# One transposed half tile copied out of PSUM by another engine, in a kernel whose order is set by a planner: tanh(x w1) * (x w2)

## The chip, the cores and the metric

The kernel runs on one core of a Trainium2 chip. The time is the device time of one execution in microseconds. Before the change three executions took 297.3, 297.45 and 297.87 us, so the median is 297.45 us.

In this document PE is TensorE (matmuls; PEld is its weight load), DVE is VectorE, ACT is ScalarE, POOL is GpSimd and SP is SyncE, which here only issues DMAs.

## The reference

```python
def setup_inputs():
    batch, m, k, n = 16, 512, 1024, 768
    return {
        "x": np.random.randn(batch, m, k).astype(np.float32),
        "w1": np.random.randn(k, n).astype(np.float32),
        "w2": np.random.randn(k, n).astype(np.float32),
    }

def reference(x, w1, w2):
    y1 = np.matmul(x, w1)
    y2 = np.matmul(x, w2)
    return (np.tanh(y1) * y2).astype(np.float32)
```

There are 8192 rows of x (64 row tiles of 128), a depth of 1024 (8 slices of 128, in two halves of 4), and 2 x 768 columns of weights. The weights are seen as three blocks of 512 columns: block a is the first 512 columns of w1, block b the first 512 of w2, and block g holds the last 256 of w1 and the last 256 of w2 side by side.

## The kernel before

**Two ways of multiplying.** The first four row tiles (HEAD = 4) are multiplied plainly: per row tile, block and depth slice one matmul of 128 x 128 by 128 x 512 in fp16. An op named `m2a3` is row tile 2, block a, slice 3. The other 60 row tiles go in 20 groups of three ("triples"). Three row tiles in two depth halves, times three blocks in two halves, would take 18 products of four matmuls each; the kernel takes 15, from sums and differences of halves of x (ops `S..`, on VectorE) and of halves of the weights (ops `B..`, on VectorE, made once). A product is an op like `p6.0`, product 6 of triple 0; each has four matmuls, and copies (`copy..`, `seed..`, on ScalarE) and additions (`add..`, on VectorE) join the products in PSUM. Tanhs (`th..`, `t..`) are on ScalarE and the final multiplications (`mu..`, `m0.i` to `m2.i`, `mh..`) on VectorE.

**How data comes in.** At the start SP and ScalarE issue loads of x and of the weights as fp32 into staging space (`arena`, `early_x`), and GpSimd loads block b and later x straight into fp16. Casts to fp16 follow: `ca0` to `ca7` (block a, VectorE), `cg0` on VectorE and `cg1` to `cg7` on ScalarE (block g), `cx20` (row tile 2, half 0) and so on (VectorE). The weight loads of block g come behind those of x and block a on SP's queue; one pair of them serves both `cg0` and `cg4`.

**How x is transposed.** From row tile 7 on, a DMA does it (line 387). The first seven row tiles are transposed by TensorE: op `PT20` is row tile 2, half 0, four matmuls against an identity (line 380) into a PSUM bank. Then `e20` copies the bank to `xT` (lines 366 on ScalarE and 368 on VectorE), and `m2a0` and its like can read it. Row tile 3 has a tile of its own, `xT_kept`; the first halves of row tiles 0 and 1 are transposed in fp32.

**Other work.** `D0` to `D63` on ScalarE (line 390) sum the absolute values of each row tile; each is an ACTIVATE followed by a read-out of the sum. `f1` to `f5` near the end test all those sums for a range: `f1` to `f3` on VectorE, one small matmul `f4` (line 495), and `f5` on VectorE; if they fail a general path runs, which they don't here. POOL and SP order x loads, transposing DMAs and stores.

**What sets the order.** Nothing is scheduled on the chip: each engine runs its queue in order. The queues are written by a planner (class `Planner`, lines 75 to 223) when the program is built. Every op has one cost per engine that may run it, a due time and the ops it needs; the planner walks through time, gives each op to an engine and a PSUM bank when both are free, and the order in which it does so is the program's order. The order of the products on TensorE is fixed by a list; all else follows from the costs. A change of one cost can therefore change which engine takes another op, which bank it gets and in which order the queues stand.

The costs of the copies that this change touches are in `by_pe` (line 587), called for each half of the first seven row tiles.

Of the kernel before, what the change touches and what calls it, by code (L numbers as in the profile page):

```python
# [74 lines left out]
class Planner:  # L75
# [9 lines left out]
    def op(self, name, engines, due, needs, fn, *args, behind=(), issued=(), chains=(), xfer=0.0, latency=None, seeds=False,  # L85
           lands=None, hold=0.0):
        assert name not in self.ops, name
        self.ops[name] = dict(engines=engines, due=due, needs=[n for n in needs if n], behind=[n for n in behind if n], issued=[n for n in issued if n], fn=fn, args=args,
                              chains=chains, xfer=xfer, latency=latency, seeds=seeds, lands=lands, hold=hold)
        for c in chains:  # L90
            self.chains.setdefault(c, {"left": 0, "bank": None, "end": 0.0, "act": 0.0, "dve": 0.0})["left"] += 1
# [135 lines left out]
def kernel(  # L227
# [16 lines left out]
    HEAD = 4  # L244
# [66 lines left out]
    op = plan.op  # L311
# [245 lines left out]
    for n, what in enumerate(by_pool):  # L557
# [7 lines left out]
        else:  # L565
            mt, h = int(what[1]), what[2:]
# [20 lines left out]
    def by_pe(mt, h, due, load):  # L587
        fp32 = (mt, h) in FP32
        op(f"PT{mt}{h}", {"pe": 0.44 if fp32 else 0.24}, due, [load], transpose_pe, mt, h, ("T", mt, h), chains=[("T", mt, h)])
        op(f"e{mt}{h}", {"dve": 0.6 if fp32 else 0.45, "act": 0.5} if mt < HEAD else {"act": 0.5}, due + 0.4, [f"PT{mt}{h}"], evacuate, mt, h, ("T", mt, h),  # L590
           chains=[("T", mt, h)])

    for n, after in enumerate(("PT00", "PT10")):
# [1 line left out]
    for mt in range(HEAD):  # L595
        for h in range(2):
            if (mt, h) not in FP32:
                op(f"cx{mt}{h}", {"dve": 0.37}, lands[f"x{mt}{h}"] - 1, [f"Lx{mt}{h}"], cast_x, mt, h)
            by_pe(mt, h, lands[f"x{mt}{h}"] - 2, f"Lx{mt}{h}" if (mt, h) in FP32 else f"cx{mt}{h}")
        op(f"D{mt}", {"act": 1.05}, START + 8, [f"Lx{mt}0", f"Lx{mt}1"], abs_x, mt, hold=11 + 4 * mt)  # L600
    for mt in rows[HEAD:BY_PE]:
        for h in range(2):
            by_pe(mt, h, x_loads[mt, h][1] - 2 - 0.1 * h * (mt == HEAD + 1), x_loads[mt, h][0])
# [36 lines left out]
    for n, s in enumerate("agb"):  # L640
        for mt in range(HEAD):
            if (s, mt) == ("b", HEAD - 1):
                continue
            due, behind = (lambda n: landed[slices["agb".index(s) * KO + n]] + 0.8 + 0.02 * mt), []
            finals(mt, s, due(KO - 1) + (5.0, 3.0, 7.0)["agb".index(s)], plain(mt, s, due, behind))

    mt = HEAD - 1
# [57 lines left out]
    for i in range(TRIPLES):  # L705
# [10 lines left out]
        for o in C_OPS:  # L716
# [20 lines left out]
            mt = HEAD + 3 * i + r  # L737
            due = soonest[i, name] + LAST
# [177 lines left out]
```

## Time and profile before

| | |
|---|---|
| median of three executions | 297.45 us |
| the profiled execution | 297.16 us |
| its span, first to last instruction | 295.6 us |
| VectorE busy | 255.8 us |
| ScalarE busy | 224.4 us |
| GpSimd busy | 42.3 us |

The span is 1.56 us shorter than the execution's time; the rest lies around it. The profile's timeline gives, per row: the start in us from the span's start, the duration, the engine, the line of the kernel, the operation, the tiles written and read, the shape out and in, and in brackets how long the engine had been idle before it and what released it. A row with "x2" or more merges instructions that follow one another, and its duration is that of the run. VectorE and ScalarE instructions that follow one another overlap by about 0.1 us in these rows, and matmuls overlap more: a matmul of 512 columns shows 0.38 us and the next one starts 0.216 us later. A busy share of TensorE is thus the share of time in which some matmul was under way.

The copies and casts of one half row tile, 128 x 512, stand in the profile's groups with 586 to 587 ns (ACT COPY from PSUM, line 366), 425 ns (DVE COPY from PSUM, line 368) and 427 ns (DVE CAST from fp32, line 368).

### The profile page before, as it was taken

To read this page: it belongs to the slowest core of one execution; us is meant where nothing else is said; L and a number is where in the kernel's file an instruction comes from. 1 tells how busy PE (TensorE), PEld (TensorE's weight loads), DVE (VectorE), ACT (ScalarE), POOL (GpSimd) and SP (SyncE) were. 2 spreads that over 40 slices of the span, in tenths; PEclk is the share of its full clock that TensorE was granted. 3 is DMA by queue.
4 is the path that set the end of the run, shared out by engine and by line. 5 is a ranking of instruction groups with operands and counts; after the bars stand their busy time and mean duration, and the time that the engine had idled before them with its cause. 6 is when DMAs were issued, how large, how long until landed. Compare 5 with 4: busy or idle time off the path is not lost. (4 is left out here: it accounts for less than half of the span.)

```text
span 295.6 us, 4588 instructions
## 1 busy us (share of the span) xinstructions
PE 289.5 (98%) x1374; PEld 132.3 (45%) x1374; DVE 255.8 (87%) x552; ACT 224.4 (76%) x454; POOL 42.3 (14%) x94
## 2 busy tenths in 40 slices
PE   7999999999999999999999999999999999999994
PEld 3445444444444444444444444444444444444442
DVE  1679999999989998898989888898988889898875
ACT  2698599799878878877888888677777767778442
POOL 0065022202102102202012021020211100000000
PEclk9999999999999999999999999999999999999999
DMA  6999999999999999989999999999999999241234
GB/s 217 391 321 204 182 141 169 210 247 230 240 194 197 247 226 216 252 218 239 204 190 246 231 236 270 164 271 264 224 298 225 213 175 324 104 162 53 109 136 169
DMA packets 84858, 63.63 MB, mean 215 GB/s; under 512 B 62816, under 2 KB 67168, under 8 KB 84832
## 3 DMA queue, kind: packets, MB, share of 16 engines
q1 hardware_dynamic: 73888, 45.10, 59.7%
q0 software_dynamic: 9936, 16.65, 36.0%
q10 hardware_dynamic: 1008, 1.57, 1.5%
q8 instruction: 11, 0.18, 0.2%
q14 instruction: 15, 0.12, 0.1%
HBM read 39.85 MB, written 25.17 MB: 220 GB/s over the span
## 5 line engine op out<-in xcount | busy, mean ns | idle before, releaser
L457 PE MATMUL bank<-b,early_x 128*128 128x512 f16 x640 | 148.3, 379 | 0.0
L457 PEld LDWEIGHTS <-early_x 128*128 128x128 f16 x800 | 78.1, 98 | 94.3 <-DVE early_x L421 0.3
L467 DVE TENSOR_TENSOR bank<-bank,arena 128x512 f32<-128x512 f32 x100 | 69.6, 696 | 13.6 <-ACT arena L461 10.9
L461 ACT ACTIVATE arena<-bank 128x512 f32<-128x512 f32 x100 | 57.6, 596 | 18.1 <-PE bank L457 18.1
L475 DVE TENSOR_TENSOR o<-o,bank 128x256 f32<-128x256 f32 (+1 forms) x128 | 61.9, 516 | 7.3 <-ACT o L470 5.9
L390 ACT ACTIVATE junk<-xh 128x1024 f16<-128x1024 f16 x60 | 63.4, 1057 | 0.1
L457 PEld LDWEIGHTS <-xT 128*128 128x128 f16 x400 | 39.0, 98 | 46.9 <-issue 0.4
L457 PE MATMUL bank<-b,xT 128*128 128x512 f16 x240 | 58.3, 379 | 0.0
L470 ACT ACTIVATE o<-bank 128x256 f32<-128x256 f32 (+1 forms) x80 | 34.8, 438 | 26.0 <-DVE bank L467 22.8
L457 PE MATMUL bank<-wh,xT 128*128 128x512 f16 x160 | 41.0, 379 | 0.0
L457 PE MATMUL bank<-wh,early_x 128*128 128x512 f16 x160 | 40.9, 379 | 0.0
L362 POOL DMA_DIRECT2D xh<-in_x_dram x61 | 32.4, 540 | 16.6 <-ACT junk L390 8.6
L421 DVE TENSOR_TENSOR early_x<-early_x,xT 128x512 f16<-128x512 f16 x80 | 33.5, 420 | 0.5
L470 ACT ACTIVATE o<-arena 128x512 f32<-128x512 f32 x40 | 25.2, 629 | 7.5 <-DVE arena L467 7.5
L501 POOL CAST held<-xT 128x1 f32<-128x1 f16 x18 | 4.5, 251 | 161.3 <-DMA xT<-xh 161.3
L461 ACT ACTIVATE bank<-bank 128x512 f32<-128x512 f32 x40 | 21.4, 570 | 4.7 <-PE bank L457 3.9
L430 PE MATMUL bank<-wh,xT 128*128 128x512 f16 x72 | 19.5, 379 | 0.3
L467 DVE TENSOR_TENSOR arena<-bank,arena 128x512 f32<-128x512 f32 x20 | 13.7, 686 | 3.6 <-ACT arena L461 3.6
L421 DVE TENSOR_TENSOR early_x<-xT,xT 128x512 f16<-128x512 f16 x40 | 16.7, 418 | 0.0
L421 DVE TENSOR_TENSOR early_x<-xT,early_x 128x512 f16<-128x512 f16 x40 | 16.7, 418 | 0.0
L467 DVE TENSOR_TENSOR bank<-arena,bank 128x512 f32<-128x512 f32 x20 | 13.8, 692 | 0.1
L390 ACT ACTIVATE junk<-wh 128x768 f16<-128x768 f16 x16 | 13.6, 847 | 0.1
(51 smaller groups left out, 140.0 us busy)
## 6 DMA issues: line engine op xcount, KB each, us to landing
out_dram<-o SPq DMA_DIRECT2D x59, 384.0 KB, 5.1
xh<-in_x_dram POOLq DMA_DIRECT2D x58, 256.0 KB, 6.7
arena<-in_w_dram SPq DMA_DIRECT2D x12, 256.0 KB, 5.6
early_x<-in_x_dram SPq DMA_DIRECT2D x8, 256.0 KB, 4.9
arena<-in_w_dram ACTq DMA_DIRECT2D x4, 256.0 KB, 5.9
wh<-in_w_dram POOLq DMA_DIRECT2D x8, 128.0 KB, 5.5
xT<-xh SPq DMA_TRANSPOSE x57, 4.2
out_dram<-o SPq DMA_DIRECT2D x3, 256.0 KB, 2.5
```

Source lines behind the costliest of these rows:

```text
L362: pin(nc.gpsimd.dma_start(xh(mt)[:, cols], xf[mt][:, cols]))
L390: pin(nc.scalar.activation(junk[:, :src.shape[-1]], src, ACT.Abs, scale=scale, accum_out=sums[:, column:column + 1]))
L421: pin(engine[e].tensor_tensor(x_operand(i, v), x_operand(i, a), x_operand(i, b), OP[how]))
L430: pin(nc.tensor.matmul(bank(chain)[:, :rhs.shape[-1]], xt(mt)[:, k, :], rhs, start=first, stop=k == KO - 1, skip_group_check=True))
L457: pin(nc.tensor.matmul(place(i, dst), x_operand(i, a)[:, k, :], w_rhs(b, k), start=begins and k == 0, stop=k == KH - 1, skip_group_check=T ...
L461: pin(nc.scalar.activation(place(i, dst), place(i, src), ACT.Copy, scale=float(sign)))
L467: pin(nc.vector.tensor_tensor(place(i, dst), a, b, ALU.add if signs == (1, 1) else ALU.subtract))
L470: pin(nc.scalar.activation(out_tile(HEAD + 3 * i + r)[:, lo:lo + n], place(i, src)[:, :n], ACT.Tanh, scale=float(sign)))
L475: pin(nc.vector.tensor_tensor(o, o, place(i, src)[:, at:at + n], ALU.mult))
L501: pin(nc.gpsimd.tensor_copy(held, xt(mt)[:, 0, :1]))
```

## The change

In `by_pe`, the copy `e20` may run on VectorE only, with cost 0.45; the other copies of the first four row tiles count ScalarE's time with 0.6 in place of 0.5. The copies of row tiles 4 to 6 stay on ScalarE with 0.5.

```diff
     def by_pe(mt, h, due, load):
         fp32 = (mt, h) in FP32
         op(f"PT{mt}{h}", {"pe": 0.44 if fp32 else 0.24}, due, [load], transpose_pe, mt, h, ("T", mt, h), chains=[("T", mt, h)])
-        op(f"e{mt}{h}", {"dve": 0.6 if fp32 else 0.45, "act": 0.5} if mt < HEAD else {"act": 0.5}, due + 0.4, [f"PT{mt}{h}"], evacuate, mt, h, ("T", mt, h),
+        op(f"e{mt}{h}", {"dve": 0.45} if (mt, h) == (2, 0) else {"dve": 0.6 if fp32 else 0.45, "act": 0.6} if mt < HEAD else {"act": 0.5}, due + 0.4, [f"PT{mt}{h}"], evacuate, mt, h, ("T", mt, h),
            chains=[("T", mt, h)])
```

The order that the planner then writes differs in these places:

| engine | before | after |
|---|---|---|
| VectorE, start | cx20 ca2 cx30 ... ca7 e31 cg0 | cx20 ca2 **e20** cx30 ... ca7 cg0 |
| ScalarE, start | e10 e20 e30 e01 e60 e11 D0 copy376.0 e21 D1 tha0 cg4 tha1 tha2 cg1 cg5 tha3 cg2 cg6 cg3 cg7 D2 thg0 ... thg3 D3 e61 e40 e41 | e10 e30 e01 e60 e11 D0 e21 copy376.0 **e31 cg4 tha0** tha1 cg1 cg5 tha2 cg2 cg6 tha3 cg3 cg7 D1 thg0 ... thg3 D2 e61 **D3** e40 e41 |
| TensorE, start | m2a0 PT30 m2a1 m2a2 m0a3 PT01 m3a0 m1a3 m3a1 PT60 m3a2 PT11 m2a3 m3a3 m0a4 p7.0 | m2a0 m2a1 PT30 m2a2 m0a3 PT01 m1a3 m2a3 m3a0 PT60 m3a1 m3a2 PT11 m3a3 p7.0 m0a4 |
| TensorE, end of block a | m2a6 m0a7 m1a7 m3a4 m3a5 m3a6 m2a7 m3a7 | m2a6 m0a7 m1a7 m2a7 m3a4 m3a5 m3a6 m3a7 |
| VectorE, first triple | B29.0 S3.0 S34.0 S11.0 S35.0 add64.0 S15.0 | B29.0 **B48.0** S3.0 S34.0 S11.0 S35.0 add64.0 S15.0 |
| TensorE, first triple | m0b7 p6.0 p1.0 p12.0 m1b7 m2b7 p9.0 | m0b7 **m1b7** p6.0 p1.0 p12.0 m2b7 p9.0 |
| TensorE, near the end | p13.18 f4 p6.19 p10.19 p4.18 p5.18 p9.19 | p13.18 p6.19 p10.19 p4.18 p5.18 **f4** p9.19 |
| VectorE, near the end | f1 S34.19 f2 S35.19 f3 add60.18 f5 m0.18 add312.19 m2.18 add64.19 add8.18 | S34.19 f1 add60.18 S35.19 m2.18 m0.18 add312.19 add64.19 f2 f3 add8.18 f5 |

Beside these, neighbours change places in some triples (such as t2 with copy60, or m0 with add312), the PSUM banks of the chains are handed out differently from the first triple on (the product p10.0 takes the bank that e40 leaves, before it took that of e41), and on SP's queue the store of row tile 4 stands before the transposing DMA of row tile 16. GpSimd's queue is the same.

## The prediction

> **What bounds the kernel now.** I read the page's totals first, then a window over the long middle, then the timeline of single engines around the edits.
>
> ```profile
> span 295.6 us, 4588 instructions
> PE 289.5 (98%) x1374; PEld 132.3 (45%) x1374; DVE 255.8 (87%) x552; ACT 224.4 (76%) x454; POOL 42.3 (14%) x94
> 17.66:291.43 273.77, 273.67 (x1290) 124.81 (x1288) 247.53 (x531) 214.89 (x439) 41.62 (x88) 1.00 0.99 210
> ```
>
> The window row gives, from its left, the length of the stretch, TensorE's busy time (matmuls), weight loads, VectorE, ScalarE, GpSimd, the granted clock (1.00). From 17.66 us to its last matmul TensorE is idle for 0.10 us of 273.77. So TensorE bounds the kernel, and nothing after 17.66 can give back more than a few tenths. The edits lie before that, and they can matter in two ways only: by moving the moment at which the gapless stretch begins, or by opening holes in it.
>
> **The edit itself: e20 to VectorE, e31 back to ScalarE.** The built order has row tile 2's first copy (e20) on VectorE, between two casts; row tile 3's second copy (e31) goes the other way. Each engine keeps its count of copies.
>
> ```profile
> 8.34 0.43 DVE L368 CAST wh<-arena 128x512 f16<-128x512 f32 x1
> 8.46 0.23 PEld L380 LDWEIGHTS <-xh 128*128 128x128 f16 x4 [0.52 <-DVE xh L368]
> 8.90 0.59 ACT L366 COPY xT<-bank 128x512 f16<-128x512 f16 x1 [1.12 <-PE bank L380]
> 9.33 0.43 DVE L368 CAST xh<-early_x 128x512 f16<-128x512 f32 x1 [0.57 <-DMA early_x<-in_x_dram]
> 9.54 0.10 PEld L430 LDWEIGHTS <-xT 128*128 128x128 f16 x1 [0.62 <-ACT xT L366]
> 9.81 0.23 PEld L380 LDWEIGHTS <-xh 128*128 128x128 f16 x4 [0.18 <-DVE xh L368]
> 10.66 0.25 PEld L380 LDWEIGHTS <-xh 128*128 128x128 f16 x4 [0.29 <-DVE xh L368]
> 14.72 0.10 PEld L430 LDWEIGHTS <-xT 128*128 128x128 f16 x1 [0.21 <-issue]
> 15.25 0.10 PEld L430 LDWEIGHTS <-xT 128*128 128x128 f16 x1 [0.44 <-ACT xT L366]
> 15.98 0.42 DVE L368 COPY xT_kept<-bank 128x512 f16<-128x512 f16 x1
> 17.18 0.43 DVE L368 CAST wh<-arena 128x512 f16<-128x512 f32 x1 [0.78 <-DMA arena<-in_w_dram]
> 17.43 0.38 PE L430 MATMUL bank<-wh,xT_kept 128*128 128x512 f16 x1
> 17.66 1.24 PE L430 MATMUL bank<-wh,xT 128*128 128x512 f16 x5
> ```
>
> Row 8.90 is e20 on ScalarE, 0.59; row 15.98 is the same copy on VectorE (e31), 0.42. VectorE is idle from 8.77 to 9.33, waiting for row tile 3's data. So e20 runs there 8.90 to 9.32, and the cast behind it (row 9.33, cx30) is not delayed. The first matmul of row tile 2 (row 9.54) starts 0.16 earlier, at 9.38.
>
> Does 0.16 reach the end? In the new order one more matmul of row tile 2 stands ahead of the transposes PT30: two matmuls of 0.216 (five starts in 1.24 with 0.38 for the last) fill 9.38 to 9.81, where PT30 may start as before. Then two matmuls to 10.48, and PT01 needs the cast cx01 and cannot load before 10.66. Before, the spare matmul filled this hole and PT01 came at 10.70. So 0.04 is left of 0.16. It stays 0.04 through 15.25 (e21, now 0.04 earlier). TensorE would finish the first weight block at 17.60 instead of 17.65 (17.43 + 0.216). But the first matmul of the next block needs the cast cg0: row 17.18, which waited 0.78 for a weight load, ends 17.61, and the matmul comes at 17.66. The loads are unchanged and wait for no copy. **Head: 0**; between -0.02 (the matmul at 17.65 plus no wait) and +0.16 (the hole at 10.48 grows by the whole gain and nothing behind absorbs it). I take 0, since row 17.66 follows cg0 by the 0.05 that a released TensorE needs.
>
> [...]
>
> **e31 and the reordered ScalarE queue.** ScalarE now does e31, then the cast cg4, and only then the tanh of row tile 0.
>
> ```profile
> 16.55 0.60 ACT L433 ACTIVATE o<-bank 128x512 f32<-128x512 f32 x1 [0.30 <-PE bank L430]
> 17.17 0.62 ACT L366 CAST wh<-arena 128x512 f16<-128x512 f32 x1
> 17.69 1.08 ACT L433 ACTIVATE o<-bank 128x512 f32<-128x512 f32 x2
> 19.72 0.59 ACT L433 ACTIVATE o<-bank 128x512 f32<-128x512 f32 x1
> 21.72 1.14 ACT L366 CAST wh<-arena 128x512 f16<-128x512 f32 x2 [0.39 <-DMA arena<-in_w_dram]
> ```
>
> PT31 starts 15.43; a copy starts 0.42 behind its transposes (26.13 to 26.55, below): e31 15.85 to 16.44. Its reader, one matmul later in the order, starts 16.73: 0.24 spare. cg4 uses the same load as cg0, so it starts at 17.17 as now, and ScalarE idles 0.7 ahead of it. The displaced tanh takes 17.69; the tanhs behind it move one place each, so the casts cg1, cg5, cg2, cg6 keep their places, and the last tanh falls into the 0.39 of idle time before 21.72. **Cost 0**; without that idle time it would be one tanh's 0.5.
>
> **Two sums of absolute values and one weight sum move up.** ScalarE's D3 now stands between e61 and e40, and VectorE's B48.0 between B29.0 and S3.0.
>
> ```profile
> 25.10 1.05 ACT L390 ACTIVATE junk<-early_x 128x1024 f16<-128x1024 f32 x1
> 26.13 0.39 PE L380 MATMUL bank<-ident_h,xh 128*128 128x128 f16 x4
> 26.55 0.59 ACT L366 COPY xT<-bank 128x512 f16<-128x512 f16 x1 [0.31 <-PE bank L380]
> 27.68 1.07 ACT L366 COPY xT<-bank 128x512 f16<-128x512 f16 x2 [0.54 <-PE bank L380]
> 30.09 0.59 ACT L366 COPY xT<-bank 128x512 f16<-128x512 f16 x1 [0.51 <-PE bank L380]
> 26.21 1.29 DVE L412 TENSOR_TENSOR b<-wh 128x1024 f16<-128x1024 f16 x2
> 28.02 0.69 DVE L412 TENSOR_TENSOR b<-b,b 128x1024 f16<-128x1024 f16 x1
> 28.79 0.43 DVE L421 TENSOR_TENSOR early_x<-xT 128x512 f16<-128x512 f16 x1
> 29.13 0.42 DVE L421 TENSOR_TENSOR early_x<-xT,xT 128x512 f16<-128x512 f16 x1
> 29.61 0.76 DVE L421 TENSOR_TENSOR early_x<-early_x,xT 128x512 f16<-128x512 f16 x2
> 30.88 0.42 DVE L421 TENSOR_TENSOR early_x<-early_x,xT 128x512 f16<-128x512 f16 x1
> 28.80 1.02 PE L457 MATMUL bank<-wh,xT 128*128 128x512 f16 x4
> 31.40 0.38 PE L457 MATMUL bank<-b,early_x 128*128 128x512 f16 x1
> 35.93 0.42 DVE L421 TENSOR_TENSOR early_x<-xT 128x512 f16<-128x512 f16 x1 [0.28 <-DMA xT<-xh]
> ```
>
> D3 starts 0.48 behind e61 (two copies in 1.07), at 27.03, and holds ScalarE 1.05: e40 starts 28.08 instead of 27.68, ends 28.67; e41 ends 29.15. The product p10.0 (row 28.80) used e41's bank with no time to spare; in the new assignment it takes e40's, free at 28.72. So it starts at 28.80 still. e50 keeps 30.09.
>
> VectorE: B48.0 starts 28.62 (two such sums take 1.29, so 0.60 apart) and S3.0, which needs e41, at 29.22 instead of 28.79. From S3.0 to S15.0 (row 30.88) the rows show 2.09. Of this 0.14 is a wait for the copy e51 at row 29.61 (ops of this kind start 0.34 apart, 28.79 and 29.13), and it is gone when S3.0 is late. So S15.0 starts 29.22 + 1.95 = 31.17 and ends 31.59; p6.0 can start 31.64. TensorE has m1b7 moved ahead of p6.0, 31.40 + 0.216 = 31.62. **Stall 0.02 to 0.03.** Bounds: 0 if VectorE runs a hair faster, and 0.42 if S15.0 is late by B48.0's whole 0.69 (31.30 + 0.69 + 0.05 - 31.62). I take 0.03, which the spacing of the rows gives. The remaining 0.29 of VectorE's lateness ends at 35.93, where it now idles 0.28.
>
> [...]
>
> **The flag near the end.** The one-matmul check f4 moves behind p5.18, its input f3 behind VectorE's add64.19.
>
> ```profile
> 272.95 0.24 DVE L492 TENSOR_REDUCE count<-good 128x1 bf16<-128x80 f32 x1
> 273.56 0.70 DVE L467 TENSOR_TENSOR bank<-bank,arena 128x512 f32<-128x512 f32 x1 [0.37 <-ACT o L470]
> 276.02 0.68 DVE L467 TENSOR_TENSOR arena<-arena,bank 128x512 f32<-128x512 f32 x1
> 273.59 0.17 PE L495 MATMUL bank<-count,ones 128*128 128x8 bf16 x1
> 275.34 2.97 PE L457 MATMUL bank<-b,early_x 128*128 128x512 f16 x13
> ```
>
> TensorE reaches f4 at 275.34 + 8 x 0.216 - 0.03 = 277.04. add60.18 (row 273.56) waited for a ScalarE tanh on its bank; in the new program order it precedes that tanh, so VectorE is 0.6 ahead. A 0.34 sum comes in between it and add64.19, f5's 0.1 goes out, so add64.19 starts about 275.7; f2 and f3 behind it end 1.0 later, at 276.7. **Cost 0.** If add60.18 still waits, add64.19 starts 276.3, f3 ends 277.3, and TensorE waits 0.3.
>
> The other swaps repeat orders that this trace already runs without a hole in other triples; one store moves ahead of one transposing DMA on SP's queue, GpSimd's order is the same. I cost them at nothing, covered by the gapless row above.
>
> **Sum.** 0 + 0 + 0.03 + 0 = 0.03 on the profiled execution's 297.16, giving 297.19. That execution stands 0.29 below the median 297.45, to which the same 0.03 gives 297.48: **297.5**.
>
> **Rivals.**
> Slower: D3 in front of e40. If D3's place costs all of its 1.05 and its read-out's 0.2 instead of the 0.40 worked out, e41 ends at 28.75 + 1.24 = 29.99, S3.0 starts 30.03, S15.0 ends 32.40 and p6.0 waits until 32.45: a hole of 0.83, 298.3. It decides from S15.0 ending after 32.16, 0.57 later than worked out. For it: e40, e41, S3.0, S15.0 and p6.0 hang on one another and p6.0 has nothing to spare. Against it: ScalarE's 0.54 of idle time at row 27.68 covers half of D3.
> Flag: TensorE waits 0.3 in front of f4, 297.75; against it stands the new program order.
> Copy: e20 takes ScalarE's 0.59 on VectorE also, cx30 comes 0.16 late, and no later wait absorbs it: 297.6; against it row 15.98.
> Gain kept: cg0's load lands 0.2 earlier and the 0.16 arrives, 297.3. Nothing in the edit moves a load.
> [...]
> Faster: cg0's load lands most of a microsecond earlier, and the head's holes become worth closing. The weight-load idle times 0.62, 0.18, 0.21 and 0.44 above sum to 1.45; about half lies beside running matmuls, an estimate from matmuls of 0.38 that start 0.216 apart, so 0.7: 296.75.
>
> **How the numbers follow.** Forecast 0.63 (its own range 297.2 to 297.8), flag 0.06, copy 0.04, gain kept 0.05, full drain 0.02, slower chain 0.15, faster 0.05. About 0.2% (0.6 us: below 296.86 or above 298.04) is what a measurement of this kernel can tell from no change; its three runs spread over 0.57. So faster 0.05, same 0.80, slower 0.15. The range 297.0 to 298.1 takes in the five middle cases with that spread and leaves out the two outer ones, 2 in 10.
>
> **What would show it.** e20 on VectorE at 8.9, 0.42 long; TensorE's first matmul on the second weight block still at 17.66; S15.0 ending 31.6 and p6.0 at 31.65; f3 ending before 277.0; TensorE's idle time from 17.66 on still about 0.1. A hole over 0.3 anywhere behind 17.66, or cg0 at another time than 17.2, makes the prediction wrong.

## The result and the profile after

The changed kernel takes 298.56 us (median of 22 executions) against 297.27 us for the kernel before (also 22); the ratio is 1.0032 with a 95% interval of 1.0020 to 1.0044. It is slower by 0.3%. The forecast was 297.5 us and, with a chance of 0.80, no change that a measurement can tell.

The median hides how the executions lie. Of the 22, seven took 296.98 to 297.61 us, fourteen took 298.37 to 299.46, and one 301.74. The seven have a mean of 297.29, the time of the kernel before; the fourteen have a mean of 298.74. Fourteen of 21 with a loss of 1.45 make 0.97 us, which is the 0.3%. So the question is what costs some executions 1.4 us and spares the others.

The profiled execution took 298.81 us. These are its totals and its window from the second weight block's first matmul to the last matmul; its timeline around the edits follows.

```profile
span 297.3 us, 4587 instructions
PE 289.8 (97%) x1374; PEld 132.9 (45%) x1374; DVE 256.1 (86%) x552; ACT 223.8 (75%) x454; POOL 42.6 (14%) x94
17.84:291.54 273.70, 273.59 (x1290) 124.93 (x1288) 247.64 (x531) 215.59 (x441) 41.66 (x88) 1.00 0.99 210
```

```profile
9.33 0.42 DVE L368 COPY xT<-bank 128x512 f16<-128x512 f16 x1 [0.58 <-PE bank L380]
9.67 0.42 DVE L368 CAST xh<-early_x 128x512 f16<-128x512 f32 x1
16.10 0.58 ACT L366 COPY xT_kept<-bank 128x512 f16<-128x512 f16 x1 [0.20 <-PE bank L380]
17.09 0.62 ACT L366 CAST wh<-arena 128x512 f16<-128x512 f32 x1 [0.41 <-DMA arena<-in_w_dram]
17.62 1.08 ACT L433 ACTIVATE o<-bank 128x512 f32<-128x512 f32 x2
27.16 1.06 ACT L390 ACTIVATE junk<-early_x 128x1024 f16<-128x1024 f32 x1
28.21 1.55 ACT L366 COPY xT<-bank 128x512 f16<-128x512 f16 x3
31.25 0.42 DVE L421 TENSOR_TENSOR early_x<-early_x,xT 128x512 f16<-128x512 f16 x1
31.73 1.47 PE L457 MATMUL bank<-b,early_x 128*128 128x512 f16 x6
277.14 0.17 PE L495 MATMUL bank<-count,ones 128*128 128x8 bf16 x1
```

The stretch is as full as before: TensorE is idle for 0.11 of 273.70 us (0.10 of 273.77 before). The copy e20 is on VectorE and takes 0.42 (9.33), D3 stands ahead of e40 (27.16, 28.21), S15.0 ends at 31.67 and p6.0 starts at 31.73, and f4 (277.14) stands in a run of matmuls without a hole. TensorE's last matmul starts at 291.16; before, at 291.05. Of the 1.65 us between the two profiled executions, 0.10 lies there. The rest must lie behind the last matmul, where the last stores are issued and land.

These are the DMA views of two short windows: 285 to 290.5 us, ahead of the last matmul, and 291.5 to 297 us, behind it. The rows of queues give the number of packets, MB and the share. "q8 instruction" and "q14 instruction" are two queues by the names that the view gives them; what their packets carry it does not say. ScalarE's stores are on q10, SP's on q1. The rows of stores end with the median time from issue to landing; the GB/s row has 40 equal slices. The kernel before, both windows:

```profile
q1 hardware_dynamic: 390, 0.86, 41.1%
q8 instruction: 1, 0.02, 1.4%
```

```profile
GB/s 0 60 0 0 119 387 343 402 402 291 350 350 321 343 350 336 343 313 105 15 0 0 0 0 0 0 0 0 0 0 0 0 60 0 0 0 0 0 0 0
q14 instruction: 2, 0.02, 1.1%
out_dram<-o ACTq DMA_DIRECT2D x1, 256.0 KB, 2.3
out_dram<-o SPq DMA_DIRECT2D x2, 128.0 KB, 2.3
out_dram<-o ACTq DMA_DIRECT2D x1, 128.0 KB, 2.3
```

The changed kernel, the same windows:

```profile
q1 hardware_dynamic: 368, 0.82, 38.4%
q14 instruction: 1, 0.01, 0.9%
```

```profile
GB/s 105 22 22 22 22 238 387 417 343 357 358 313 350 440 328 335 313 328 239 8 7 7 7 7 15 15 22 30 22 22 22 0 0 0 0 0 0 0 0 0
q8 instruction: 1, 0.02, 1.2%
out_dram<-o ACTq DMA_DIRECT2D x1, 256.0 KB, 2.3
out_dram<-o SPq DMA_DIRECT2D x2, 128.0 KB, 3.9
out_dram<-o ACTq DMA_DIRECT2D x1, 128.0 KB, 3.9
```

The last three stores are issued at the same distance from the last matmul in both (0.5, 0.9 and 1.2 us behind it), but land after 3.9 us instead of 2.3. Their bulk moves at the same 300 to 400 GB/s; then a remainder trickles at 7 to 30 GB/s for 1.6 us. And one packet has changed sides. The last of the eleven packets on q8, over by 287.8 in the kernel before, runs from 293.32 to 294.38 in the changed one, among the last stores.

The remainder itself is telling. This is the changed kernel between 294.2 and 296 us:

```profile
DMA packets 27, 0.02 MB, mean 14 GB/s; under 512 B 3, under 2 KB 27, under 8 KB 27
q1 hardware_dynamic: 18, 0.02, 4.1%
q10 hardware_dynamic: 9, 0.01, 1.3%
```

Three of the 27 packets are under 512 bytes. The other 24 carry 1 KB each: in the order of their times eight on q1 (SP's first store), eight on q10 (ScalarE's) and eight on q1 (SP's second), which is one sixteenth of each of the three 128 KB stores. They go in single file, and the first of them starts at 294.36, as the q8 packet ends. In the kernel before the last 24 packets run beside one another and need 0.27 us, here 1.42.

The packets on q8 keep step with TensorE: the eleven are 0.18 MB together, 16 KB each, they come at intervals of 22 to 34 us in every trace, TensorE starts about 250 instructions between one and the next (202 at the first and 2478 at the tenth in the changed kernel), and an instruction added to its queue or taken out goes with another place of the last of them, as the experiments show. The expectations below speak of them as TensorE's instruction fetches; the queue's name and these numbers fit that, but no trace names the engine that they serve or what they carry. Ten of the eleven open no hole in TensorE's gapless stretch, which in the changed kernel is idle for 0.11 us in all.

Why did the packet move? TensorE's queue in the built program has 2761 instructions before and 2760 after: same matmuls and weight loads, one wait fewer. The traces agree: of TensorE's semaphore instructions they hold 23 and 22. (The page's totals, 4588 and 4587, are a net sum: ScalarE has three instructions fewer, VectorE three more, TensorE one fewer.) So the theory, F where the expectations name it, is: **the edit itself costs nothing; TensorE's queue is one instruction shorter, with that the last q8 packet comes more than 6 us later, among the last stores, and the end comes 1.4 to 1.6 us later.** The rivals are that the new order delays the end in some other way (other banks, a store moved ahead of a transposing DMA, ScalarE's or VectorE's order near the end), and that one half of the edit does it.

### The profile page after: what moved, and what is told of

Same layout as the page of the kernel before. It is cut to its first block, busy times and chain, and to the rows that moved or that the text cites. A ratio compares the mean times of both kernels' runs of the same rounds, so it can differ in the third digit from the quotient of the medians.

```text
span 297.3 us, 4587 instructions
## 1 busy us (share of the span) xinstructions
PE 289.8 (97%) x1374; PEld 132.9 (45%) x1374; DVE 256.1 (86%) x552; ACT 223.8 (75%) x454; POOL 42.6 (14%) x94
```

## The experiments

This table gives for each kernel TensorE's queue length in the built program, where the last q8 packet starts in the profiled execution relative to the start of the last matmul, how long the last three stores take to land, and the time. All in us; "ratio" is to the kernel before on the same chip, with its 95% interval.

| kernel | queue | last q8 packet | last stores land | median | ratio |
|---|---|---|---|---|---|
| before | 2761 | -4.43 | 2.3 | 297.27 | |
| changed | 2760 | +2.16 | 3.9 | 298.56 | 1.0032 [1.0020, 1.0044] |
| changed, one more filler matmul | 2762 | -4.51 | 2.1 to 2.2 | 297.21 | 1.0000 [0.9991, 1.0009] |
| before, one filler matmul fewer | 2759 | +0.61 | 3.0 | 298.94 | 1.0059 [1.0046, 1.0073] |
| only e20 on VectorE | 2760 | +1.44 | 3.7 | 299.19 | 1.0073 [1.0059, 1.0087] |
| only the cost of 0.6 | 2761 | -4.50 | 2.4 to 2.5 | 298.0 | 1.0025 [1.0015, 1.0034] |
| before, without f4 | 2759 | +2.13 | 3.7 | 298.92 | 1.0051 [1.0028, 1.0073] |
| only e20, one more filler | 2762 | -4.50 | 2.1 to 2.2 | 297.64 | 1.0002 [0.9983, 1.0020] |
| before, one more filler | 2763 | -4.42 | 2.2 to 2.9 | 297.2 | 0.9986 [0.9967, 1.0004] |

**The changed kernel with a longer TensorE queue.** One more filler matmul of 64 columns goes in at the very start, while TensorE waits for its first data; with its weight load it adds two instructions.

```diff
-    WARM = 512, 512, 512, 512, 512, 512, 512
+    WARM = 512, 512, 512, 512, 512, 512, 512, 64
```

> The changed kernel with one more warm-up matmul of 64 columns at the start, where TensorE waits for x, so TensorE's queue is two instructions longer (2762 instead of 2760; before it was 2761) and nothing else moves. Theory F (the last 16 KB instruction fetch, q8, slips behind TensorE's last matmul and into the landing of the last stores, because the queue is one instruction shorter): the last q8 packet starts near 287 us again, the last store lands 2.3 us after its issue, time as before the change, ratio 0.999 to 1.001. Theory O (the new order of copies, sums and flag costs the time): still slower, ratio about 1.003. Theory H (the head starts the gapless stretch 0.2 us later and that is all there is): ratio about 1.0006 with the stores' landing unchanged.

It takes 297.21 us, ratio 1.000: the loss is gone, with every edit of the change still in and only TensorE's queue longer. The last q8 packet is back ahead of the last matmul, and the stores land after 2.2 (first row from the window 285 to 290.5, second from 291.5 to 297):

```profile
q8 instruction: 1, 0.02, 1.4%
```

```profile
out_dram<-o SPq DMA_DIRECT2D x3, 128.0 KB, 2.2
```

Its profiled execution was not typical: it took 299.72, one of the slowest of the twelve, because of a single hole in which TensorE waited for a transposing DMA:

```profile
105.25 1.04 PE L457 MATMUL bank<-wh,xT 128*128 128x512 f16 x4 [2.51 <-DMA xT<-xh]
```

Of the eleven other executions eight took 296.86 to 297.24 and cannot have had it. A second profiled execution of this kernel was to check that.

> The changed kernel with the added warm-up matmul once more, since its profiled execution was one of the slowest of twelve, by a hole at 102 us. Theory F: last q8 packet near 287 us, landing 2.1 to 2.3 us, no hole of over 0.3 us after 18 us, about 297.2.

That was missed: 298.86 us. There was no hole at 105, but another one at 163, where ScalarE waited for a store to free its buffer and TensorE for ScalarE:

```profile
163.17 1.15 ACT L470 ACTIVATE o<-arena 128x512 f32<-128x512 f32 x2 [2.75 <-DMA out_dram<-o]
```

```profile
164.85 1.02 PE L457 MATMUL bank<-wh,early_x 128*128 128x512 f16 x4 [1.62 <-ACT bank L461]
```

The end behaved as the theory says (q8 packet at -4.46, landing 2.2). Both holes are single events in the middle of the program; what makes them was not followed.

**The kernel before with a shorter TensorE queue.** First by leaving out one of the filler matmuls between the transposes:

```diff
-        for cols in FILL:
+        for cols in FILL[:2] if chain == ("f", 1) else FILL:
```

> The kernel before with the last of the three filling matmuls behind PT10 left out (it computes nothing that is used), so TensorE's queue has 2759 instructions and the order is that of before. Theory F: the last q8 packet starts behind TensorE's last matmul, about 293 us, the last three stores land 3.9 us after their issue instead of 2.3, most runs near 298.6, ratio 1.002 to 1.005. Theory O: no change, ratio 0.999 to 1.001. Theory H: no change, or 0.1 us if the filling matmul kept the clock up.

298.94, and the last q8 packet moves behind the last matmul (+0.61) with the stores at 3.0. Both numbers miss the expectation: the ratio of 1.0059 lies above 1.005, and 3.0 is less than 3.9. This run doesn't prove the theory either: TensorE came to full clock only at 10.38 us (5.42 in the kernel before) and its last matmul started 1.78 later, at 292.83, so the start of this execution was another one too; whether the edit made it so, one profile does not show. A cleaner way to shorten the queue is to take out f4, the one-matmul check near the end, which leaves start and order alone. f5 then tests the count of one partition directly, so the range test no longer covers all partitions.

```diff
-        pin(nc.tensor.matmul(bank("flag")[:, :8], ones.bitcast(bf16)[:, 1:2 * P:2], count.to_broadcast([P, 8]), start=True, stop=True))
+        pass
...
-        pin(nc.vector.tensor_scalar(bad, bank("flag")[:, :1], float(P * n_sums) * 2.0 ** -12, None, ALU.not_equal))
+        pin(nc.vector.tensor_scalar(bad, count, float(n_sums), None, ALU.not_equal))
```

> The kernel before without the one small matmul f4, so that the range test no longer covers the sums of all partitions (f5 compares each partition's own count). TensorE's queue has 2759 instructions, the start is untouched, and nothing after f5 depends on the flag before the end. Theory F: the last q8 packet starts behind TensorE's last matmul and the last three stores land late, so 0.7 to 1.7 us more in most runs, ratio 1.002 to 1.006, with TensorE's last matmul at 291.0 as before. Rival N (the loss of the earlier shortened queue came from its start alone, where TensorE ran at half clock until 10.4 us): ratio 0.999 to 1.001.

The kernel before, with less work, is slower by 0.5%. Its last matmul starts at 290.97, earlier than in the kernel before, and the loss is behind it, in the same form as in the changed kernel (window 291.5 to 297):

```profile
GB/s 0 0 60 74 283 387 357 372 350 320 328 469 320 350 306 328 320 127 30 7 7 15 15 22 22 22 30 22 0 0 0 0 0 0 0 0 0 0 0 0
q8 instruction: 1, 0.02, 1.0%
out_dram<-o SPq DMA_DIRECT2D x2, 128.0 KB, 3.7
```

This kernel has none of the change's order and its stores land late all the same; the changed kernel with the filler has all of that order and they land early. So the rivals that lie in the new order are out as causes of the 1.4 us. One of its twelve executions took 297.37. The remaining doubt was that any edit of the kernel before might do this; lengthening its queue instead of shortening it speaks against that.

> The kernel before with the added warm-up matmul of 64 columns: 2763 instructions in TensorE's queue. Theory F: nothing changes, since the last q8 packet was early already; ratio 0.999 to 1.001, last q8 packet near 287 us. If the added matmul itself shortened the start (clock at full rate sooner), the ratio would lie below 0.999 and the recovery seen with it in the changed kernel would not be the fetch's alone.

297.2 us, ratio 0.9986 with 1 inside the interval, q8 packet at -4.42: the filler matmul by itself neither costs nor gains, and among the kernels measured the late q8 packet goes with the queues of 2759 and 2760 instructions only.

One thing stays open here. The kernel before has long executions too: on the chip of "without f4" five of 23 took 298.07 to 299.98 us, on this one two of 17 took 298.96 and 299.87, and the only one on the chip of the last profiles took 298.35. None of them was profiled, so it isn't known whether a late q8 packet or a hole in the middle, as above, made them long.

**Each half of the change alone.** First e20 on VectorE with ScalarE's cost left at 0.5, then the cost of 0.6 with e20 free to go to either engine.

```diff
-{"dve": 0.6 if fp32 else 0.45, "act": 0.5} if mt < HEAD
+{"dve": 0.45} if (mt, h) == (2, 0) else {"dve": 0.6 if fp32 else 0.45, "act": 0.5} if mt < HEAD
```

> Only the first part of the edit: e20 on VectorE, ScalarE's copies still counted with 0.5. TensorE's queue has 2760 instructions. Theory F: slow as the whole change, ratio 1.002 to 1.005, last q8 packet about 293 us. Theory O: some part of the loss, between 1.000 and 1.003, and the stores land as before.

```diff
-{"dve": 0.6 if fp32 else 0.45, "act": 0.5} if mt < HEAD
+{"dve": 0.6 if fp32 else 0.45, "act": 0.6} if mt < HEAD
```

> Only the second part of the edit: ScalarE's copies of the first four row tiles counted with 0.6, e20 free to go to either engine. TensorE's queue has 2761 instructions, as before the change. Theory F: ratio 0.999 to 1.001 unless TensorE's gapless stretch has new holes, last q8 packet about 287 us. Theory O: some part of the loss, between 1.000 and 1.003.

Both are slower, for different reasons. With e20 alone the ratio of 1.0073 lies above the 1.005 that was expected: the queue has 2760 instructions and the last q8 packet is late (+1.44); besides, p6.0 starts 0.51 us behind the matmul ahead of it, 0.29 more than the usual 0.216, and the last stores go out 0.36 later against the last matmul. With 0.6 alone the queue keeps its 2761 instructions, the last q8 packet is early (-4.50), the stores land after 2.4 to 2.5, and the loss is a hole in front of p6.0, in the place that the prediction's slower rival named:

```profile
32.47 1.90 PE L457 MATMUL bank<-b,early_x 128*128 128x512 f16 x8 [0.42 <-DVE early_x L421]
```

From the start of the matmul ahead to p6.0's it is 0.80, 0.58 more than 0.216, and the last matmul starts 0.76 later than before. So neither half gives the order that both together give, where p6.0 waits 0.04. The loss of the e20 half can be split by lengthening its queue with the same filler as above:

> The first part of the edit alone with the added warm-up matmul of 64 columns: 2762 instructions. Theory F: the last q8 packet is back near 287 us and the stores land in 2.1 to 2.3 us; what stays is the hole of 0.3 us in front of p6.0 and the last store's issue 0.36 us later, so 297.7 to 298.1, ratio 1.001 to 1.003, against 1.0073 without the added matmul. Rival N: ratio stays near 1.007.

297.64 us: 1.55 less than the median without the filler, which was measured on another chip. The hole at p6.0 (0.28) and the later stores (0.36) stay. They add up to 0.64, and the profiled execution is 0.62 longer than that of the kernel before, but the medians on that chip are only 0.25 apart: time and ratio lie just below the forecast, and the interval takes in no difference.

**The changed kernel again.** Its own profile could have been a chance one, and the seven executions at 297.3 were still without an explanation.

> The changed kernel once more, for the place of the last q8 packet and the landing of the last stores in another execution. Theory F: the packet starts behind TensorE's last matmul again; if the time is near 297.2, the packet lies outside the landing of the last stores, and if it is near 298.6, inside.

> The changed kernel a third time, to meet one of its executions near 297.2. Theory F: with 297.2, the last three stores land 2.1 to 2.5 us after their issue, and the last q8 packet either started before TensorE's last matmul or after the stores had landed; with 298.5, as in the first profile.

> The changed kernel a fourth time. Theory F: near 297.2 with the last three stores landing 2.1 to 2.5 us after their issue, or near 298.5 with 3.7 to 3.9 us, as in the first profile.

These took 299.16, 298.45 and 298.54 us. Each has the last q8 packet at +2.15 to +2.37 and the stores at 3.7 to 3.9; their last matmuls start at 291.49, 290.99 and 291.00. Two of them thus finish TensorE's work before the kernel before does (291.05), and are still 1.2 and 1.3 us slower than its median.

> The changed kernel once more. A third of its executions took about 297.2 us and no profile has shown one of these. Late fetch as the whole cause: where this execution takes about 298.5, TensorE's last instruction packet starts 2.1 to 2.4 us behind its last matmul and the last three stores land 3.7 to 3.9 after their issue; where it takes about 297.2, that packet is over before the last stores are issued, or it starts late too but leaves the stores alone, and they land after 2.1 to 2.5. The rival, something ahead of the last matmul: in an execution of 297.2 the stores land late all the same, and the last matmul starts over a microsecond earlier than at 291.0.

> As for the look before this one: either 298.5 with the stores landing 3.7 to 3.9 after their issue, or 297.2 with 2.1 to 2.5; the last matmul at 291.0 to 291.3 in both.

> As for the two looks before: either 298.5 with the stores landing 3.7 to 3.9 after their issue, or 297.2 with 2.1 to 2.5; the last matmul at 291.0 to 291.3 in both.

> As for the three looks before: either 298.5 with the stores landing 3.7 to 3.9 after their issue, or 297.2 with 2.1 to 2.5; the last matmul at 291.0 to 291.3 in both.

The times are 298.47, 298.66, 297.03 and 298.81. The third is one of the group that escapes. Its window from the second weight block's first matmul on, and the DMA views of the two windows (285 to 290.5, then 291.5 to 297):

```profile
17.60:291.30 273.70, 273.64 (x1290) 124.78 (x1288) 247.80 (x531) 215.78 (x442) 41.39 (x88) 1.00 1.00 210
```

```profile
q8 instruction: 1, 0.02, 1.1%
```

```profile
GB/s 67 52 45 82 320 395 343 417 365 313 343 343 343 350 335 343 357 187 0 0 0 0 0 0 0 0 0 0 0 0 0 0 60 0 0 0 0 0 0 0
out_dram<-o SPq DMA_DIRECT2D x2, 128.0 KB, 2.2
out_dram<-o ACTq DMA_DIRECT2D x1, 128.0 KB, 2.2
```

Its last matmul starts at 290.97, within 0.05 of those that took 298.45 to 298.66 (290.99 to 291.02). What differs is the last q8 packet: 289.32 to 290.32, 1.65 ahead of the last matmul and over before the last stores are issued; no trickle follows, and they land after 2.2. In the other three the packet starts at +1.3 to +2.1 and they land after 3.7 to 3.9; the +1.3 is earlier than the 2.1 to 2.4 that was expected, and the stores land late all the same. The rival, that the escaping executions gain ahead of the last matmul, is out for the one that was profiled.

So within one program the last q8 packet can come on either side of the last matmul, and a late packet and late stores go together in all seventeen profiles: ten with the packet at +0.6 to +2.4 and the last stores landing after 3.0 to 3.9, seven with it at -4.5 to -1.65 and 2.1 to 2.9.

What ties the late stores to the q8 packet is not shown; the order of the packets is. In nine of the ten late profiles (all but the kernel before with one filler matmul fewer) the last 24 packets are again eight of each of the three stores, in single file (in one of them with a few others beside the first). In seven of these nine the file starts within 0.1 us of the q8 packet's end; in the two whose q8 packet starts at +1.3 and +1.4 it starts 1 us behind it, after a few 2 KB packets of the 256 KB store that was issued before. None of the early profiles ends with such a file of 24. The traces do not name what carried a packet, so what puts these 24 one behind another stays open.

Why the q8 packet comes late stays open too. It is not a slide by one instruction, which would be some 0.1 us (an estimate: a matmul and its weight load together take 0.216). In all seventeen profiles the first ten packets come at nearly the same places in TensorE's queue, the tenth when 2475 to 2489 of its 2775 to 2779 traced instructions have started. The early eleventh comes at 2718 to 2745, the late one only at 2771 to 2773, behind the start of TensorE's last branch. What decides between the two, and why a third of the changed kernel's executions escape, no run shows.

## Why the prediction was wrong

**The edit: right.** e20 takes 0.42 on VectorE. In the execution of 297.03, whose clock rose at the same moment as before (5.41 and 5.42), the copy runs 8.82 to 9.24 and the head comes out nearly as worked out: TensorE's first matmul on the second weight block follows the cast cg0 by 0.05, as before. The last matmul of the first block starts at 17.31, 0.12 earlier than before, where the prediction left 0.04 of the gain, and waiting for cg0 takes it back. The matmul behind it starts at 17.57 instead of 17.66, because cg0 itself starts 0.09 earlier. In the first profile that matmul came at 17.84, against the forecast's 17.66, and cg0 (over at 17.54) no longer bound it: there TensorE reached full clock at 7.33 and the transposes came later. The prediction gave "cg0 at another time than 17.2" as a sign of its failure; that sign is of a tenth or two and decided nothing.

The step "head: 0" rested on the rows at 17.18 and 17.66 before, and the runs go with them: in six of the eight profiles of the changed kernel that matmul follows cg0 by 0.05; in the other two, 0.24 and 0.29 behind cg0, the head is later for another reason.

**ScalarE's queue: right.** e31 at 16.10, cg4 at 17.09, the tanhs from 17.62; cg4 had waited 0.41 for its load, so e31 ahead of it cost nothing.

**The sums that move up: right.** Forecast: S15.0 ends at 31.59, p6.0 at 31.64, stall 0.02 to 0.03. Measured in the execution with the same clock start: 31.48 and 31.54, stall 0.04; in the first profile 31.67 and 31.73, stall 0.04. The other executions of the changed kernel reach 0.08. No run shows the case of full drain (0.02 of the chances): VectorE's sums there, of 0.68 each, start 0.60 to 0.61 apart in the first profile (27.34, 27.95 and 28.55, the last of them B48.0), as the row at 26.21 had it. The slower rival (D3's whole cost) did not come about here, but it is real: the cost of 0.6 alone opens a hole of 0.58 at that place.

**The flag: right.** f4 starts at 276.95 and 277.14 with no hole around it, and f3 ends at 276.92 in the first profile, ahead of the 277.0 that the prediction allowed.

**The sum: wrong, by a term that it does not contain.** The step that failed is the sentence that the edits "can matter in two ways only", by moving the start of the gapless stretch or by opening holes in it. There is a third: what lies behind the last matmul. "0 + 0 + 0.03 + 0 on the profiled execution's 297.16" takes that part as it was, at nothing and without a reason. The measured terms are +0.10 at the last matmul (-0.08 to +0.43 in the other seven profiles of the changed kernel) and +1.55 behind it. The prediction compared what each engine runs and in which order; it did not count the instructions of the queues, where one wait fell out of TensorE's, nor look at the eleven packets of "q8 instruction" and ask where the last one would be. All its rivals lay ahead of the last matmul, the range, 297.0 to 298.1, was built from these alone, and so was its list of signs: TensorE's idle time of 0.11 and f3 ahead of 277.0 came out as it said, while the time did not. For the third of the executions that took about 297.2 the forecast holds: 297.29 on the mean, against 297.5. The one such execution that was profiled had the early q8 packet (-1.65).

## What to carry to other kernels

When an edit leaves the bounding engine's work unchanged and the time moves all the same, compare the end first: when the last matmul starts, when the last stores are issued, and how long they take to land. Look there at the queues that the profile calls "instruction" too: here the ends of the changed kernel with a q8 packet among the last stores took 1.4 to 1.6 us more, as much as seven matmuls of 0.216, and two idle instructions in TensorE's queue, at a place where it waits anyway, moved the packet away in both kernels where that was tried. Count each engine's instructions, waits included, and measure an edit of a few tenths with the queue length held constant, or the place of that packet is measured with it.

## What the runs showed of the hardware that was not expected

- With one instruction fewer in TensorE's queue (2761 to 2760) the last q8 packet starts 1.3 to 2.4 us behind the last matmul in seven of eight profiles of the changed kernel, and 1.65 us ahead of it in the eighth; in the kernel before it starts 4.4 us ahead. By their times, two thirds of the changed kernel's executions have it late (an estimate from 14 of 21 at 298.37 us and more).
- With a q8 packet of 16 KB among the last stores (128 KB each) these land 1.4 to 1.7 us later (0.7 later where it starts only 0.6 behind the last matmul), though the packet takes 0.9 to 1.3 us itself. With a packet of 8 KB on q14 among the same stores less was seen: in the kernel before it starts 0.6 us behind the last matmul, takes 0.6, and the stores land after 2.3; with one more filler it starts there too, takes 0.8, and one of the three stores lands after 2.9, the others after 2.2 and 2.55. In the new order it comes 0.5 to 1.1 us ahead of the last matmul, and there the two stores issued 1.6 and 1.3 us ahead of it land after 2.7 to 3.2 instead of 2.1; in the first profile no instruction behind them waits for them.
- TensorE reaches its full clock between 4.8 and 7.3 us from the start of the span in executions of the same kernel (4.82, 4.95, 5.41, 5.79, 6.49, 6.88, 6.89 and 7.33 in the eight of the changed kernel; in the first profile, that of 7.33, a matmul of 512 columns shows 0.63 us at 6.61 and 0.38 at 8.17). The gapless stretch starts at 17.57 to 17.88 us in these, a spread of twice what the edit was about, but the clock is not its only cause: the two latest starts (17.87 and 17.88) follow cg0 by 0.05, which itself ends 0.2 us later there than in the kernel before; in those with full clock at 6.88 and 7.33 TensorE starts 0.24 and 0.29 behind cg0.
